# Four 32-partition DMAs in place of one broadcast load, and four in place of one store, in a decoder layer's delta-rule stage

## The chip, the cores and the metric

One core of a Trainium2 chip. The metric is the device time of one execution in microseconds (us), lower is better. The program is one decoder layer for a prompt of 4096 tokens and eight decode tokens. The engines are PE (matrix multiply), DVE (vector), ACT (scalar), POOL, and SP, which here does nothing but issue DMAs. Sixteen DMA engines carry them.

## The reference, cut to what matters

The part that the change touches is the chunked gated delta rule of the prompt. For each chunk and head a unit lower triangular system is solved:

```python
lower = eye + beta[..., :, None] * jnp.einsum('nbhtd,nbhid->nbhti', k, k) * dec_strict
rhs = jnp.concatenate([(beta * jnp.exp(G))[..., None] * k, beta[..., None] * v], -1)
sol = lax.linalg.triangular_solve(lower, rhs, left_side=True, lower=True, unit_diagonal=True)
...
def step(s, xs):
    w_c, ut_c, aqk_c, qd_c, kd_c, gl_c = xs
    u = ut_c - jnp.einsum('bhcd,bhde->bhce', w_c, s)
    o = jnp.einsum('bhcd,bhde->bhce', qd_c, s) + jnp.einsum('bhti,bhie->bhte', aqk_c, u)
    s = gl_c[..., None, None] * s + jnp.einsum('bhcd,bhce->bhde', kd_c, u)
    return s, o
```

Around it stand a projection of the input, a short convolution, sliding-window attention, an output projection and a layer norm.

## The kernel before

The prompt is cut into 16 blocks of 256 tokens. A first phase runs over the blocks (loop variable `s`) and does the projections of q, k and v of the delta heads (PE tile `pj`, w in `w1`), the convolution (DVE, L315, into `kqv` and `vv`), the decay factors (`g`, `dec`), the triangular inverses and the recurrent state `S`. A second phase does attention, gates, output projection and layer norm; it has no instruction of the lines that the change touches.

In the first phase a block has two chunks of 128 tokens and four heads, so eight triangular matrices of 128 x 128. `front` writes them, with sign and decay, into the tile `U` (L379). Their inverses are made in two steps. `lanes` inverts the 32 diagonal sub-blocks of 32 x 32 (four in each matrix) by substitution on DVE, and `gdn_inv` puts the full inverses together from them with matrices on PE (tiles `pgi`, `V`, `XE`, `XZ`). `gdn_c` then updates `S`, through `r` (L491), `ut` (L503) and `S` (L508).

`lanes` works as follows. Four DMAs (L411) store the diagonal sub-blocks to a DRAM buffer `D1` of 32 rows (one for a sub-block, called a lane) and 4 KB. One DMA (L413) reads it back into the tile `LU` of 128 partitions. It reads the 32 rows four times: partitions 0 to 31 hold copy 0 of the 32 lanes, 32 to 63 copy 1, and so on. Each copy solves for a quarter of the 32 columns. `LV` starts as the matching columns of the identity (L415), and 31 steps of a multiply (L420, into `lt`) and an add (L422, into `LV`) do the substitution. One DMA (L424) stores `LV` to the DRAM buffer `D2`, and four DMAs (L429) load its parts as diagonal sub-blocks into `VTd`, from which L432 (ACT) and L433 (DVE) make the halves `vt16` for `gdn_inv`. In the trace `D1` and `D2` both read as `D`. All DMAs of this phase are issued by SP, in one order.

The text is written block after block, but the order of the instructions on each engine is set at build time by a scheduler, which mixes the substitution of one block with the projections of the next, the state update of the block before, and side work (weights for the second phase: `stg`, `wt`, `stt`, and the decode tokens: `stg`, `dkq`, `dt`). An engine runs its own list in that order, so an instruction that waits holds up what stands behind it. Each DMA signals on one of eight semaphores, which are used in turn.

Of the kernel before, what the change touches and what calls it, by code (L numbers as in the profile page):

```python
# [33 lines left out]
def body(ctx, tc, I, O, seq):  # L34
# [3 lines left out]
    pe, act, dve, pool, sp = nc.tensor, nc.scalar, nc.vector, nc.gpsimd, nc.sync  # L38
# [72 lines left out]
    with ExitStack() as p1:  # L111
# [148 lines left out]
        def front(s, hT, ahead):  # L260
# [109 lines left out]
            for c in range(2):  # L370
                cs = slice(c * 128, (c + 1) * 128)
                for hp in range(2):
# [8 lines left out]
                    m = 4 * c + 2 * hp  # L381
                    dve.tensor_mul(Aqk[:, m:m + 2, :], pa[:, :, 0, :], decs[c][:, 2 * hp:2 * hp + 2, :])
            vt, vt16 = lanes(s, U)
            act.activation(U16[:, 0], U, AF.Copy)
            dve.tensor_sub(U16[:, 1], U, U16[:, 0])
# [19 lines left out]
        def lanes(s, U):  # L405

            d1, d2 = D1[s % 2], D2[s % 2]
            d1v = d1.rearrange("(m b) (i t) -> b i m t", b=4, t=32)
            for b in range(4):
                bs = slice(32 * b, 32 * b + 32)  # L410
                sp.dma_start(d1v[b], U[bs, :, bs])  # L411
            LU = w1p.tile([128, 32, 32], F32, name="LU", bufs=1)
            sp.dma_start(LU.rearrange("p a b -> p (a b)"), d1[None].to_broadcast([4, 32, 1024]))  # L413
            LV = w1p.tile([128, 8, 32], F32, name="LV", bufs=1)
            dve.tensor_copy(LV.rearrange("p a b -> p (a b)"), lv0)  # L415
            lt = w1p.tile([128, 8, 32], F32, name="lt", bufs=1)
            for j in range(31, 0, -1):
                j0 = j // 4
                n = 8 - j0
                dve.tensor_mul(lt[:, j0:, 0:j], LV[:, j0:, j:j + 1].to_broadcast([128, n, j]),  # L420
                               LU[:, None, 0:j, j].to_broadcast([128, n, j]))
                dve.tensor_add(LV[:, j0:, 0:j], LV[:, j0:, 0:j], lt[:, j0:, 0:j])  # L422
            d2w = d2.rearrange("l (j c i) -> c l j i", c=4, i=32)
            sp.dma_start(d2w, LV)  # L424
            d2r = d2.rearrange("(m b) (q i) -> b q m i", b=4, i=32)
            vt = VTd
            for b in range(4):
                bs = slice(32 * b, 32 * b + 32)
                sp.dma_start(vt[bs, :, bs], d2r[b])  # L429
            vt16 = w1p.tile([128, 2, 8, 2, 32], F16, name="vt16")  # L430
            ve = vt.rearrange("p m (a b) -> p m a b", b=64)[:, :, :, 0:32]
            act.activation(vt16[:, 0], ve, AF.Copy)  # L432
            dve.tensor_sub(vt16[:, 1], ve, vt16[:, 0])  # L433
            return vt, vt16
# [1020 lines left out]
```

## Time and profile before

| | us |
|---|---|
| median of three runs | 2308.78 (2307.01 to 2318.52) |
| the profiled execution | 2309.84 |
| its span, first to last instruction | 2308.1 |
| PE busy, whole span | 2119.3 |
| DVE busy, whole span | 1834.1 |
| ACT busy, whole span | 1266.6 |
| first phase, steady part | 90 to 1170 of the span |

The profile names each group of instructions as tile written, arrow, tiles read. Idle time of an engine stands in brackets before the instruction that ended it, with the one that released it. A DMA's time in the chain of waits runs from the start of its issue to its landing (of several, from the last one's). The DMA share is the mean busy share of the 16 DMA engines, so 0.25 is four of them.

### The profile page before, as it was taken

Reading aid. Unit: us, or ns where it says so; the run is one execution under the profiler, and the core shown is the slowest. Engines: PE = TensorE matmul, PEld = TensorE weight load, DVE = VectorE, ACT = ScalarE, POOL = GpSimd, SP = SyncE. Lnnn points to the kernel's source line nnn. Section 1 sums busy time; section 2 is a strip of 40 time slices with the busy share of each in tenths; the row PEclk is TensorE's granted clock in tenths of the full one; section 3 lists DMA queues with packets and bytes.
Section 4 is the critical chain, followed back from the end, with each engine's and each line's share of the span. In section 5 each row is a group of like instructions: output and inputs, shape, how many; then the busy total and the mean of one; then the engine's idle time right before and its main releaser. Section 6 shows DMA issues by size and latency. Waiting matters only on the chain.

```text
span 2308.1 us, 48753 instructions
## 1 busy us (share of the span) xinstructions
PE 2119.3 (92%) x18287; PEld 1516.0 (66%) x18287; DVE 1834.1 (79%) x5546; ACT 1266.6 (55%) x3601; POOL 162.0 (7%) x284
## 2 busy tenths in 40 slices
PE   6988798898989898899899999999999999999997
PEld 4867677787877787787576777777545454444443
DVE  7778677888888788888767977777687788898877
ACT  6755656666666576666455666666632333434332
POOL 1111110111111011110000000000000000000000
PEclk9999999999999999999899999999999999999999
DMA  8332322323333123222334311111342343333322
GB/s 321 117 114 67 88 88 72 101 89 94 124 101 98 60 76 99 77 67 79 97 102 165 113 59 63 58 59 39 125 169 74 115 141 105 115 106 111 108 91 74
DMA packets 139757, 232.18 MB, mean 101 GB/s; under 512 B 60933, under 2 KB 73529, under 8 KB 133353
## 3 DMA queue, kind: packets, MB, share of 16 engines
q1 hardware_dynamic: 138224, 228.52, 29.5%
q8 instruction: 144, 2.36, 0.4%
q14 instruction: 93, 0.75, 0.1%
q10 hardware_dynamic: 1296, 0.55, 0.1%
HBM read 154.07 MB, written 76.09 MB: 100 GB/s over the span
## 4 chain that ended last, share of the span: by engine, by line
PE 42%; DVE 17%; DMA 7%; ACT 6%; issue 2%; SPq 1%; POOL 0%; POOLq 0%; ACTq 0%; DVEq 0%
PE pp L1040 21%; PE pj L41 9%; DMA LU<-D 3%; PE pgi L41 3%; DVE kqv L315 2%; ACT Sm L870 2%; PE po L41 2%; DVE lt L420 2%; PE tr L887 2%; DVE LV L422 1%; PE tr L41 1%; PE pS L41 1%; DMA D<-LV 1%; DVE bst L1075 1%; PE pga L41 1%
## 5 line engine op out<-in xcount | busy, mean ns | idle before, releaser
L41 PE MATMUL pj<-hT,w 128*128 128x256 f16 x4608 | 578.8, 276 | 3.4 <-ACT hT L255 2.6
L41 PEld LDWEIGHTS <-w 128*128 128x128 f16 x4800 | 452.8, 99 | 62.2 <-issue 6.8
L1040 PEld LDWEIGHTS <-S 128*128 128x128 f16 x1536 | 150.4, 99 | 170.7 <-issue 3.6
L41 PEld LDWEIGHTS <-hT 128*128 128x128 f16 x2048 | 159.8, 98 | 69.3 <-issue 2.0
L41 PE MATMUL pj<-wq,hT 128*128 128x512 f16 x768 | 191.8, 379 | 0.0
L315 DVE SCALAR_TENSOR_TENSOR kqv<-u,cols,kqv 128x256 f32<-128x256 f32 x384 | 181.4, 478 | 2.7 <-ACT kqv L313 2.1
L1040 PE MATMUL pp<-wz,S 128*128 128x512 f16 x768 | 181.1, 382 | 0.0
L870 ACT ACTIVATE Sm<-Sm,nm 128x256 f32<-128x256 f32 (+1 forms) x256 | 125.5, 492 | 92.4 <-DVE nm L867 92.3
L1040 PE MATMUL pp<-wo,S 128*128 128x512 f16 x768 | 171.3, 379 | 0.7 <-DVE zs L1216 0.6
L420 DVE TENSOR_TENSOR lt<-LV,LU 128x60 f32<-128x60 f32 (+24 forms) x496 | 119.4, 241 | 54.9 <-DMA LU<-D 48.8
L1040 PE MATMUL pp<-wz,hT 128*128 128x512 f16 x576 | 133.0, 382 | 1.2 <-ACT zs L1127 1.2
L863 DVE CUSTOM_DVE_ANT_0 Sm<-pS,swam 128x256 f32<-128x256 f32 (+1 forms) x256 | 96.4, 415 | 35.5 <-PE tr L887 32.0
L1040 PE MATMUL pp<-wo,A 128*128 128x512 f16 x540 | 122.1, 379 | 0.0
L41 PE MATMUL pj<-wkv,hT 128*128 128x256 f16 x768 | 107.7, 275 | 0.4 <-ACT v L814 0.4
L1040 PEld LDWEIGHTS <-hT 128*128 128x128 f16 x612 | 60.1, 99 | 72.7 <-issue 4.4
L422 DVE TENSOR_TENSOR LV<-LV,lt 128x60 f32<-128x60 f32 (+24 forms) x496 | 102.6, 207 | 6.2
L41 PE MATMUL pga<-kqv 128*128 128x256 f32 x256 | 75.3, 409 | 25.7 <-DVE kqv L322 25.7
L1079 POOL TENSOR_TENSOR rs<-rs,cf 128x1 f32<-128x1 f32 (+1 forms) x33 | 22.8, 692 | 1077.1 <-DVE rs L1078 1077.1
L1040 PEld LDWEIGHTS <-A 128*128 128x128 f16 x540 | 52.9, 99 | 62.0
L1021 ACT ACTIVATE S<-zt 128x512 f16<-128x512 f32 x64 | 40.2, 630 | 85.3 <-DVE zt L1027 81.1
L1134 ACT ACTIVATE zs<-zs 128x512 f32<-128x512 f32 x48 | 30.2, 629 | 100.5 <-DVE zs L1133 100.5
L315 DVE SCALAR_TENSOR_TENSOR vv<-u,cols,vv 128x256 f32<-128x256 f32 x192 | 82.6, 479 | 1.7 <-ACT vv L313 0.9
(378 smaller groups left out, 4607.0 us busy)
## 6 DMA issues: line engine op xcount, KB each, us to landing
hT<-hD SPq DMA_DIRECT2D x32, 1024.0 KB
x<-in_xT_dram SPq DMA_DIRECT2D x32, 512.0 KB
hD<-hT SPq DMA_DIRECT2D x16, 1024.0 KB
x<-in_x_prompt_dram SPq DMA_DIRECT2D x60, 256.0 KB
out_y_prompt_dram<-x SPq DMA_DIRECT2D x60, 256.0 KB
stg<-in_ws_dram SPq DMA_DIRECT2D x16, 512.0 KB
LU<-D SPq DMA_DIRECT2D x16, 512.0 KB
wS<-wt SPq DMA_DIRECT2D x16, 512.0 KB
```

The lines of the kernel that those rows point to most:

```text
L41: pe.matmul(out, l, r, start=st, stop=sp_)
L315: dve.scalar_tensor_tensor(d, u[:, b2, j:j + 256], cwj(j, blk), d, op0=ALU.mult, op1=ALU.add)
L420: dve.tensor_mul(lt[:, j0:, 0:j], LV[:, j0:, j:j + 1].to_broadcast([128, n, j]), LU[:, None, 0:j, j].to_broadcast([128, n, j]))
L422: dve.tensor_add(LV[:, j0:, 0:j], LV[:, j0:, 0:j], lt[:, j0:, 0:j])
L863: dve.tensor_tensor_reduce(Sm[:, h, k0:256], pS[:, h2, k0:256], swam[:, k0:256], 0.125, -1e30, op0=ALU.add, op1=ALU.max, accum_out=mx[:, h ...
L870: act.activation(Sm[:, h, k0:256], Sm[:, h, k0:256], AF.Exp, bias=nm[:, h:h + 1], accum_out=sm_[:, h:h + 1])
L887: pe.transpose(pt[:, h2, kb, :], Sm[:, h + h2, kb * 128:(kb + 1) * 128], ident)
L1021: act.activation(q[:, 0], src, AF.Copy)
L1040: pe.matmul(dst.rearrange("p (u c) -> p u c", c=128), A[:, hi, k, :], W[:, k // 2::2, q, wi, k % 2, :], start=new and n == 0, stop=n == 11 ...
L1075: dve.bn_stats(st[0:n, q, :], r[q][0:n])
L1079: pool.tensor_tensor(rs[0:n, 1:2], rs[0:n, 0:1], half_neg[0:n, 0:1], op=ALU.pow)
L1134: act.activation(zs, zs, AF.Silu, scale=IWS)
```

## The change

The load of `LU` and the store of `LV` each become a loop over the four copies, which issues a DMA for 32 partitions. The bytes and their places stay as they were.

```diff
             LU = w1p.tile([128, 32, 32], F32, name="LU", bufs=1)
-            sp.dma_start(LU.rearrange("p a b -> p (a b)"), d1[None].to_broadcast([4, 32, 1024]))
+            for c in range(4):
+                sp.dma_start(LU[32 * c:32 * c + 32].rearrange("p a b -> p (a b)"), d1)
...
             d2w = d2.rearrange("l (j c i) -> c l j i", c=4, i=32)
-            sp.dma_start(d2w, LV)
+            for c in range(4):
+                sp.dma_start(d2w[c], LV[32 * c:32 * c + 32])
```

Lines behind L413 move down by one, those behind L424 by two. The count of compute instructions stays; SP issues 96 DMAs more (three for the load and three for the store in each of 16 blocks). The scheduler's order changes on all engines in the first phase. In the steady part of the second it stays.

On SP, in block 11 (the one whose load stands at 858.49 us in the trace), this is the list from the store of block 10 to the load of block 11, before (`D_0_88` is `D2` of an even block, `D_1_87` is `D1` of an odd one):

```order
L424 DMA D_0_88<-LV 4x256x32
L429 DMA VTd<-D_0_88 32x8x32 x4
L411 DMA D_1_87<-U 32x8x32 x4
L413 DMA LU<-D_1_87 128x1x1024
L136 DMA x<-in_xT_dram 128x1024
```

and after:

```order
L426 DMA D_0_88<-LV 256x1x32 x4
L431 DMA VTd<-D_0_88 32x8x32 x4
L411 DMA D_1_87<-U 32x8x32 x4
L414 DMA LU<-D_1_87 32x1024 x4
L683 DMA out_delta_s_dram<-stg 128x4x128
```

The neighbours stay; one load and one store have become four each.

On DVE, the end of the list between block 11's last instruction on `U` (L379, followed by L382) and the first step of its substitution, before:

```order
L322 SCALAR_TENSOR_TENSOR vv<-th,vv 128x1024
L451 TENSOR_TENSOR VR<-V,VR 64x256
L451 TENSOR_TENSOR V_319<-pgi,V_319 64x256
L668 TENSOR_TENSOR ddl<-ddl,dbe 128x4
L669 TENSOR_TENSOR dt_12648<-xt,deg 128x4
L670 TENSOR_TENSOR doT<-ddl,dqk 128x4
L256 TENSOR_TENSOR hT<-x,hT 128x512
L671 TENSOR_TENSOR doT<-doT,dt_12648 128x4
L256 TENSOR_TENSOR hT<-x,hT 128x512
L451 TENSOR_TENSOR XZ<-pgi,XZ 64x4x64
L420 TENSOR_TENSOR lt<-LV,LU 128x31
L256 TENSOR_TENSOR hT<-x,hT 128x512
```

and after:

```order
L552 SCALAR_TENSOR_TENSOR stg<-stg,xt 128x512
L562 TENSOR_TENSOR stt<-stg 128x256
L453 TENSOR_TENSOR VR<-V,VR 64x256
L453 TENSOR_TENSOR V_319<-pgi,V_319 64x256
L562 TENSOR_TENSOR stt<-stg,stt 128x256
L562 TENSOR_TENSOR stg<-stg 128x256
L562 TENSOR_TENSOR stt<-stg,stt 128x256
L256 TENSOR_TENSOR hT<-x,hT 128x512
L453 TENSOR_TENSOR XZ<-pgi,XZ 64x4x64
L256 TENSOR_TENSOR hT<-x,hT 128x512
L493 SCALAR_TENSOR_TENSOR r<-pgi,G,Vn 128x128 x4
L421 TENSOR_TENSOR lt<-LV,LU 128x31
```

Side work (`stg`, `stt`) and the four instructions on `r`, which stood behind the first step, now stand ahead of it.

On DVE, from the last step of that substitution to the copy that starts the next `LV`, before:

```order
L422 TENSOR_TENSOR LV<-LV,lt 128x8
L315 SCALAR_TENSOR_TENSOR kqv<-u,cols,kqv 128x256 x3
L360 TENSOR_SCALAR sse<-sse 128x8
L361 TENSOR_SCALAR sc<-sse 128x8
L363 RECIPROCAL sc<-sse 128x8
L364 TENSOR_TENSOR sc<-be,sc 128x8
L365 TENSOR_SCALAR sc<-sc 128x8
L315 SCALAR_TENSOR_TENSOR kqv<-u,cols,kqv 128x256
L415 COPY LV<-cf 128x256
```

and after:

```order
L423 TENSOR_TENSOR LV<-LV,lt 128x8
L322 SCALAR_TENSOR_TENSOR kqv<-th,kqv 128x1024
L315 SCALAR_TENSOR_TENSOR vv<-u,cols,vv 128x256 x6
L379 SCALAR_TENSOR_TENSOR U<-pga,sc,dec 128x128 x2
L382 TENSOR_TENSOR Aqk<-pga,dec 128x256
L416 COPY LV<-cf 128x256
```

The convolution steps on `kqv` have moved in between the substitution's steps, and the copy has moved behind the first instructions on the next block's `U`.

## Rows read from the trace of the kernel before

**Rows 1.** Windows: length, then busy us of each engine, PE clock, DMA share, GB/s.

```profile
90.00:1170.00 1080.00, 953.73 (x9351) 820.55 (x9349) 885.43 (x3090) 668.64 (x2147) 125.11 (x224) 0.95 0.29 90
```

**Rows 2.** The chain that ended last, from 90 to 1170 us, shares by line.

```profile
by line: DMA LU<-D 6.9%; DVE kqv L315 5.3%; PE pgi L41 5.1%; DVE lt L420 3.6%; PE pj L41 3.5%; DVE LV L422 3.1%; DMA D<-LV 2.2%; issue 2.1%; PE pga L41 1.9%; DMA D<-U 1.4%; DVE wt L557 1.3%; DVE kqv L322 1.0%; SPq L411 0.7%; DVE S L508 0.7%
```

**Rows 3.** DVE's waits, 90 to 1170 us: total us, times, longest.

```profile
DVE lt L420 <- DMA LU<-D: 48.8, 14, 7.3
...
DVE LV L415 <- DMA D<-LV: 11.4, 5, 3.2
```

**Rows 4.** PE's waits, 90 to 1170 us.

```profile
PE pga L41 <- DVE kqv L322: 24.8, 15, 3.6
PE tr L41 <- DVE g L283: 19.0, 12, 2.0
PE pgi L41 <- DVE r L491: 15.2, 4, 8.6
```

**Rows 5.** SP's timeline: start us, us, issue.

```profile
586.07 0.53 SPq L413 DMA_DIRECT2D LU<-D  x1
...
650.65 0.55 SPq L413 DMA_DIRECT2D LU<-D  x1
...
855.35 1.78 SPq L411 DMA_DIRECT2D D<-U  x4
858.49 0.54 SPq L413 DMA_DIRECT2D LU<-D  x1
864.24 0.35 SPq L136 DMA_DIRECT2D x<-in_xT_dram  x1
...
993.52 0.54 SPq L413 DMA_DIRECT2D LU<-D  x1
...
1059.30 0.54 SPq L413 DMA_DIRECT2D LU<-D  x1
```

**Rows 6.** The chain that ended last, blocks 11 and 14: start us, us, piece.

```profile
856.68 1.67 DMA D<-U
...
858.49 9.41 DMA LU<-D
...
906.67 4.74 DMA D<-LV
...
1059.30 8.42 DMA LU<-D
```

**Rows 7.** Windows as in rows 1: block 14's load of LU.

```profile
1059.30:1060.80 1.50, 1.47 (x14) 1.25 (x14) 1.44 (x3) 0.73 (x2) 0.00 (x0) 1.00 0.06 14
1060.80:1062.30 1.50, 1.42 (x20) 0.91 (x18) 1.47 (x4) 1.20 (x4) 0.00 (x0) 1.00 0.24 71
...
1066.80:1068.30 1.50, 0.80 (x13) 0.51 (x11) 0.56 (x3) 0.40 (x2) 0.00 (x0) 1.00 0.02 8
```

**Rows 8.** Windows as in rows 1: block 11's four stores of U on the way.

```profile
856.60:857.10 0.50, 0.50 (x14) 0.49 (x13) 0.50 (x2) 0.50 (x3) 0.00 (x0) 1.00 0.40 66
```

**Rows 9.** DVE's timeline: first steps of four blocks' substitution, and the copy of LV.

```profile
247.00 0.21 DVE L420 TENSOR_TENSOR lt<-LV,LU 128x31 f32<-128x31 f32 x1 [7.26 <-DMA LU<-D]
391.88 0.21 DVE L420 TENSOR_TENSOR lt<-LV,LU 128x31 f32<-128x31 f32 x1 [4.88 <-DMA LU<-D]
596.20 0.21 DVE L420 TENSOR_TENSOR lt<-LV,LU 128x31 f32<-128x31 f32 x1 [4.08 <-DMA LU<-D]
867.92 0.21 DVE L420 TENSOR_TENSOR lt<-LV,LU 128x31 f32<-128x31 f32 x1 [2.63 <-DMA LU<-D]
911.43 0.29 DVE L415 COPY LV<-cf 128x256 f32<-128x256 f32 x1 [1.23 <-DMA D<-LV]
1002.42 0.21 DVE L420 TENSOR_TENSOR lt<-LV,LU 128x31 f32<-128x31 f32 x1 [1.25 <-DMA LU<-D]
```

**Rows 10.** PE's timeline behind block 11's two stalls.

```profile
869.27 1.93 PE L41 MATMUL pgi<-r,V 128*128 128x128 f32 x8 [2.02 <-DVE r L491]
915.32 1.13 PE L41 MATMUL pga<-kqv 128*128 128x256 f32 x4 [1.65 <-DVE kqv L322]
```

## The prediction

> **What bounds the kernel now.** First the place. The changed lines run only in the first phase, so I read the views from 90 to 1170 us alone. There PE is busy 953.7 of 1080 us and DVE 885.4 [rows 1]: neither is full. PE's 126 idle us (1080 - 953.7) are all that the end can gain while the amount of work and the clock stay.
>
> Second, who is late. The chain that ended last gives 6.9% of this stretch, 75 us, to the load of LU, and 2.2%, 24 us, to the store of LV [rows 2]. At the durations of one, told below, that is about eight of the sixteen loads and five of the stores: in the others something else was later. DVE's largest wait is for the load of LU, 48.8 us in 14 stalls, longest 7.3; it waits 11.4 us in five stalls for the store [rows 3]. PE's largest waits are for DVE: 24.8 us for kqv, 19.0 for g, 15.2 for r, 59.0 together [rows 4].
>
> Third, one block. In block 11 the four stores of U are issued from 855.35 on, LU's load from 858.49 to 859.03, and it lands 9.41 us after its issue began [rows 5, 6]. DVE has other work until 2.63 us before the landing, then stands; PE stands 2.02 us for r, which is behind that first step in DVE's list [rows 9, 10]. At the substitution's end the store takes 4.74 us from issue to landing [rows 6]; DVE waits 1.23 us of it at the copy into LV, and PE a little later 1.65 us for kqv, which is behind that copy [rows 9, 10].
>
> **The change part by part.**
>
> *The load.* Now it costs 9.41 us from the start of its issue to its landing in block 11, 8.42 in block 14 [rows 6]. Block 14's has little beside it: the DMA share is 0.24 from 1060.8 on and the load is over soon after 1066.8 [rows 7]. So four of sixteen engines carry it, for about 6.0 us of data; the other 2.4 are issue, start and completion. The access has four copies outermost, one for each of these engines.
>
> After, four pieces have 32 partitions outermost. The nearest rows are the four stores of U, also 32 partitions each: the last is issued 856.68 - 855.35 = 1.33 us after the first and lands 1.67 us after that [rows 5, 6], with a share of 0.40 on the way, so more than four engines [rows 8]. Low end: all engines carry the data, 6.0/4 = 1.5 us, a quarter of it behind the last issue: 1.33 + 1.67 + 0.4 = 3.4 us. Middle: only 0.40 of the engines, 6.0 x 0.25/0.40 = 3.8 us of data, with the 2.4 of before 6.2 us. High end: no engine is gained, 9.4 + 1.3 = 10.7 us. I take 4 to 4.5, near the low end, because a piece of LU has 32 runs of 4 KB, where the stores of U have short ones: a saving of 5 (at 6.2 us still 3.2).
>
> The Trainium skill, page "DMA: Bandwidth & Descriptors", section "Why a DMA increments its semaphore by 16 and not by 1", says that a DMA runs on the largest number of engines up to 16 that divides the outermost sizes of both sides. That gives four for the old load, as the share of 0.25 shows, and sixteen for each piece; no run here has yet shown the sixteen. By it alone the load would cost the low end's 3.4 us.
>
> What the saving is worth on DVE: a stall can give back no more than itself. The longest, 7.26 us, keeps 2.3; the next, 4.88, and the other twelve go [rows 9]. That is 48.8 - 2.3 = 46.5 us; with a saving of 3.2 it would be about 39. The new order puts side work and the four r instructions ahead of the first step, which covers even the slow price; I add nothing for it, since the load is in time without it.
>
> *The store.* Now 4.74 us. After, four issues and a landing like the stores of U: 1.33 + 1.67 to 2, so 3.2 us, 1.5 saved. The new order also puts kqv, six convolution steps and the next U between the last step and the copy into LV. I count 8 of the 11.4 us of rows 3; the bounds are none and all.
>
> *SP.* 96 more issues at 0.45 are 43 us of SP's time. They cost nothing here: after block 11's load SP issues nothing until 864.24 [rows 5], and the store, like the loads of VTd behind it, waits for the substitution and not for SP. If that cover were gone, the three further issues of the load would hold the DMA behind them back by 1.35 us.
>
> *The order.* The substitution's first steps stand later on DVE, its last step stands closer to the next block's U, and the half vt16 (L435) has moved behind more of the U instructions. Count and kind of compute instructions stay, so this has no price of its own; it can only make waits (rival below).
>
> *The sum.* DVE is freed of 46.5 + 8 = 54.5 us. PE's recoverable time is the 59.0 us for which it names a late DVE. The end gains only where the one falls into the other. In block 11 it does: stalls of 2.63 + 1.23 on DVE, and right behind them 2.02 + 1.23 (of the 1.65) on PE, 84%. But PE's wait for r comes in four blocks of sixteen only [rows 4], and the periods speak for less: the block with a stall of 4.08 takes 650.65 - 586.07 = 64.6 us, one with a stall of 1.25 takes 1059.30 - 993.52 = 65.8 [rows 5, 9]. So between none and 54.5 I take 0.6, 33 us. Profiled execution: its own time of 2309.8 - 33 = 2276.8; the median of three runs stands 1.1 below that execution, so 2276 is predicted. Clock changes are left out: it was 0.95 in this stretch, and I have no row that ties it to these stalls.
>
> **The rivals.**
>
> *Hidden.* The freed DVE time is given back as waits for PE, which is busy 88% of the stretch as it is [rows 1]. For it: the two periods above. Against it: PE's largest waits all name DVE. Gain 10 us or less, about 2302.
>
> *No more engines.* The pieces run as slowly as the one load did, or the four readers of one 4 KB row wait for each other at the source. Then the load is at 10.7 us, 1.3 later, and the new order's cover takes that up: 2305 to 2312. Against it: the 0.40 in rows 8.
>
> *One after the other.* A piece begins only when the one ahead is done. With 2.4 us of issue, start and completion and 0.4 of data each, the load is 4 x 2.8 = 11.2 us, and the store 4 x 1.7 = 6.8, 2 more than now. The load's 1.8 more lie under the new cover; the store's 2 on every block, behind which copy, VTd and inverse wait, give 16 x 2 x 0.6 = 19 at the most, so about 2320. It decides from the point where the pieces land more than some 2 us apart. Against it: the stores of U land 1.67 us after the last issue, so their starts and completions overlap. The same page of the Trainium skill, section "Rules for kernel authors", says not to split a transfer by partitions, because the parts serialize on the same engines, and to use one 128-partition transfer. The trace shows no such thing for the four stores of U.
>
> *A late inverse.* This is slower than before. The substitution now ends closer to the next U, and behind it come store, load of VTd, vt16 and the matrices of the inverse, on which r and S of the block wait. From the substitution's last step to VTd's landing I count 3.2 for the store and as much as the stores of U, 3.0, for the four loads: 6.2 us. If DVE and PE reach vt16 and the inverse before that, a new stall stands where LU's was. At 5 us for each block (more than the 3.5 mean of LU's stalls), and the same weight: 0.6 x (80 - 54.5) = +15, about 2324. It decides from 3.5 us for each block on. Against it: the copy into LV is covered now, and DVE has two or three more groups on U to do before vt16.
>
> **How the numbers follow.** Half a percent, 11.5 us, is about what a measurement of this kernel tells from no change. Chances: my forecast 0.70 (2245 to 2297), hidden 0.16, no more engines 0.04, one after the other 0.04, a late inverse 0.06. The lower end of the range, 2240, is all of the 54.5 us and some more of the chain's 99; the upper, 2307, leaves out the two slower cases and a part of the hidden one's scatter. Faster is 0.70 and a little of the hidden case, 0.71; slower is 0.10 with the last two, less what of them stays within the bound, 0.09; same is the rest, 0.20.
>
> **What would show each step.** Right: LU<-D in the chain at 1.7 to 3 us for its last piece instead of 9.4, a DMA share far over 0.25 while it lands, DVE's wait for LU under 5 us in total, D<-LV at about 2 us, PE's waits for g, kqv and r clearly below 59. Wrong: a DVE wait for LU of the old size (engines), or no such wait with PE's waits unchanged in sum (hidden), or a new row at vt16, XE or V in DVE's waits of over 50 us (late inverse). If the first phase gets shorter by much more than 54.5 us, the clock or the order did it, and my sum has missed its cause.

## The result and the profile after

| | us | |
|---|---|---|
| before, median of 4 runs | 2309.13 | 2307.01 to 2318.52 |
| after, median of 4 runs | 2236.32 | 2233.91 to 2240.11 |
| ratio, 95% interval | 0.968 | 0.965 to 0.971 |
| after, profiled execution | 2235.32 | span 2233.5 |

The kernel became faster by 73 us, more than twice the 33 us of the forecast and 3.7 us below the lower end of its range. Where did it come from? I cut the span where SP issues its first `wz<-wS`, a load of the second phase's weights that all kernels here have. It stands at 1204.94 us before and at 1134.84 us after. Two stretches up to it, and the one behind it up to the first issue of `wo<-wS`, follow as windows with the columns of rows 1 (length; busy us of PE, of PE's weight loads, of DVE, ACT and POOL, each with its count of instructions; PE clock, DMA share, GB/s). First the kernel after:

```profile
90.00:1100.00 1010.00, 933.60 (x9316) 801.26 (x9314) 878.93 (x3082) 668.63 (x2149) 126.68 (x224) 0.98 0.30 96
...
90.00:1134.84 1044.84, 967.54 (x9660) 827.38 (x9658) 903.77 (x3159) 686.28 (x2212) 129.70 (x227) 0.98 0.30 95
...
1134.84:1582.95 448.11, 436.02 (x4852) 312.63 (x4851) 339.49 (x1271) 281.32 (x843) 0.00 (x0) 0.99 0.21 79
```

The kernel before, for the last two:

```profile
90.00:1204.94 1114.94, 987.86 (x9692) 845.72 (x9690) 908.31 (x3163) 685.55 (x2211) 128.24 (x227) 0.96 0.29 89
...
1204.94:1658.57 453.63, 437.73 (x4835) 314.09 (x4833) 338.94 (x1269) 280.54 (x844) 0.00 (x0) 0.98 0.22 78
```

The first stretch of rows 1 (up to 1170, now up to 1100) does nearly the same work: 9351 PE instructions before [rows 1], 9316 now. Up to `wz<-wS` the phase is shorter by 1114.94 - 1044.84 = 70.1 us. PE's idle time there fell from 127.1 (1114.94 - 987.86) to 77.3 us (1044.84 - 967.54), which is 49.8 us. The other 20.3 us are PE's *busy* time, 987.86 against 967.54 at a granted clock that went from 0.96 to 0.98. The instructions recorded, 9692 and 9660, differ by 0.3%, which is some 3 us of it at the most. Behind the cut 5.5 us more are gained (453.63 - 448.11), 3.8 of them less idle PE. Together that is 75.6 us; the spans differ by 2308.1 - 2233.5 = 74.6, so in what lies outside both stretches 1.0 us is lost.

The chain that ended last, from 90 to 1100 us, beside rows 2 (the view cuts the line off):

```profile
by line: PE pgi L41 12.2%; DVE kqv L315 11.4%; PE pj L41 11.0%; DVE lt L421 6.7%; PE pga L41 6.0%; DVE LV L423 5.6%; issue 4.2%; DVE kqv L322 2.9%; PE xt L41 2.8%; DVE vv L315 2.1%; DMA x<-in_xT_dram 2.1%; ACT junk L392 1.8%; PE tr L389 1.6
```

No load of LU and no store of LV is left in it, behind the cut-off either. DVE's largest waits of the same stretch (total, times, longest) say it too:

```profile
DVE U L379 <- PE pga L41: 30.4, 30, 2.7
DVE kqv L322 <- ACT th L321: 8.6, 9, 1.2
...
DVE vt L435 <- ACT vt L434: 3.4, 4, 2.0
```

The two rows of rows 3, 48.8 and 11.4 us, are gone to the last. What grew is DVE's wait for PE at `U`, from 14.0 us to 30.4: a part of the freed time was given back there. The rows of before for `U` and for the half of the inverse `vt`, from 90 to 1170 us:

```profile
DVE U L379 <- PE pga L41: 14.0, 11, 2.6
...
DVE vt L433 <- ACT vt L432: 6.6, 8, 1.3
```

PE's waits of after answer to rows 4:

```profile
PE pga L41 <- DVE kqv L322: 23.2, 15, 2.3
PE tr L41 <- DVE g L283: 10.1, 8, 2.8
...
PE pgi L41 <- ACT V L452: 4.9, 10, 1.8
```

PE's wait for `r`, 15.2 us before, is no longer among the largest, and the one for `g` is halved. Rows 4 show the three largest only: all rows of that view in which PE waits for DVE sum to 96.4 us before and to 48.9 us now, and that fall of 47.5 is nearly all of the 49.8 us of idle time. Now block 11 closely, the one of rows 5 and 6. SP's timeline:

```profile
795.75 1.78 SPq L411 DMA_DIRECT2D D<-U  x4
798.87 1.71 SPq L414 DMA_DIRECT2D LU<-D  x4
801.80 0.40 SPq L683 DMA_DIRECT2D out_delta_s_dram<-stg  x1
...
846.27 2.52 SPq L426 DMA_DIRECT2D D<-LV  x4
850.19 1.82 SPq L431 DMA_DIRECT2D VTd<-D  x4
```

And windows over the load, beside rows 7:

```profile
798.80:799.80 1.00, 0.99 (x18) 0.77 (x16) 0.97 (x4) 0.23 (x1) 0.00 (x0) 1.00 0.00 0
799.80:800.80 1.00, 0.97 (x13) 0.67 (x10) 0.97 (x3) 0.73 (x2) 0.19 (x1) 1.00 0.84 266
800.80:801.80 1.00, 1.00 (x26) 0.76 (x24) 0.97 (x5) 0.97 (x2) 0.00 (x0) 1.00 0.93 250
801.80:802.80 1.00, 1.00 (x6) 0.78 (x6) 1.00 (x1) 1.00 (x4) 0.00 (x0) 1.00 0.13 26
```

The data run for 2 us at a share of 0.84 to 0.93, where the one load of before ran for 6 us at 0.24 [rows 7]; about 3 us behind the first issue (798.87 to some 801.8) they are over. DVE comes to the first step only 9 us later:

```profile
809.84 1.13 DVE L493 SCALAR_TENSOR_TENSOR r<-pgi,G,Vn 128x128 f32<-128x128 f32 x4
810.88 0.20 DVE L421 TENSOR_TENSOR lt<-LV,LU 128x31 f32<-128x31 f32 x1
```

There is no bracket of idle time at the step (beside rows 9), and PE's matrices on `r` start at 810.77 without one (beside rows 10). With 12.0 us from first issue to the step, even the 9.41 us of before would have been in time in this block; whether the order or the load took the stalls away has to be tried.

### The profile page after: what moved, and what is told of

The parts are those of the page before. It is cut to its first block, busy times and chain, and to the rows that moved or that the text cites. A ratio compares the mean times of both kernels' runs of the same rounds, so it can differ in the third digit from the quotient of the medians.

```text
span 2233.5 us, 48900 instructions
## 1 busy us (share of the span) xinstructions
PE 2098.6 (94%) x18287; PEld 1497.6 (67%) x18287; DVE 1831.9 (82%) x5546; ACT 1269.1 (57%) x3601; POOL 163.4 (7%) x284
## 4 chain that ended last, share of the span: by engine, by line
PE 53%; DVE 28%; ACT 11%; DMA 4%; issue 3%; POOL 0%; POOLq 0%; SPq 0%; ACTq 0%; DVEq 0%
PE pp L1042 21%; PE pj L41 11%; PE pgi L41 6%; DVE kqv L315 5%; DVE lt L421 3%; PE pga L41 3%; ACT Sm L872 3%; DVE LV L423 3%; PE po L41 2%; PE tr L41 2%; PE tr L889 2%; DMA x<-in_xT_dram 1%; DVE kqv L322 1%; PE xt L41 1%; PE pS L41 1%
## 5 line engine op out<-in xcount | busy, mean ns | idle before, releaser
L41 PEld LDWEIGHTS <-w 128*128 128x128 f16 x4800 | 450.0, 99 | 65.1 <-issue 11.4
```

Source lines behind the costliest of these rows:

```text
L41: pe.matmul(out, l, r, start=st, stop=sp_)
```

## The experiments

My theory at that point: the load was slow because its outermost size of 4 gave it four engines, DVE's stalls on it and on the store stopped PE, and the clock fell behind these stops. The rivals: the new order of the instructions did it; the store did it; the number of DMAs did it, not the engines. All six kernels, called e1 to e6 here, compute the whole reference. The first four ran beside a before of 2309.81 us (13 runs), the last two beside one of 2308.87 us (7 runs).

**One half of the change each.** First (e1) only the load is split.

```diff
+            for c in range(4):
+                sp.dma_start(LU[32 * c:32 * c + 32].rearrange("p a b -> p (a b)"), d1)
...
             sp.dma_start(d2w, LV)
```

> Only the load of LU is split into four DMAs of 32 partitions; the store of LV stays one DMA. Theory 'engines' (each piece runs on all DMA engines, so the load is short and DVE's stall for it goes): DVE's wait for LU under 5 us in sum, the load's last piece 1.7 to 3 us in the chain, time 2245 to 2265 us, most of the 73 us. Theory 'order' (the build-time order that four issues bring puts more work ahead of the first substitution step, whatever the load's speed): a time in the same region, so this run tells the two apart only together with the third. Theory 'store' (the store's part is worth as much as the load's): 2270 to 2285.

Measured: 2240.19 us, 0.968 of before (0.966 to 0.971). Windows and DVE's waits of this kernel:

```profile
90.00:1138.43 1048.43, 966.96 (x9686) 825.70 (x9685) 905.82 (x3164) 688.52 (x2212) 125.75 (x227) 0.99 0.30 94
```

```profile
DVE LV L416 <- DMA D<-LV: 4.2, 4, 1.8
```

By its ratio this is the gain of after (0.968 and 0.968); the 4 us between the two medians are not clear of the noise. The store, left as it was, costs DVE 4.2 us of waits and not 11.4. Then (e2) only the store is split.

```diff
             sp.dma_start(LU.rearrange("p a b -> p (a b)"), d1[None].to_broadcast([4, 32, 1024]))
...
+            for c in range(4):
+                sp.dma_start(d2w[c], LV[32 * c:32 * c + 32])
```

> Only the store of LV is split; the load of LU stays one DMA with four copies outermost. 'Engines': DVE's wait for LU stays near 49 us in sum, its wait for the store goes, time 2290 to 2304 us. 'Order': the order of the first phase is another one here too, so the time may come out anywhere from 2240 to 2310 with the load as slow as before. 'Store': 2270 to 2285.

Measured: 2293.65 us, 0.9923 (0.9902 to 0.9945).

```profile
90.00:1191.53 1101.53, 984.48 (x9646) 844.95 (x9644) 905.11 (x3151) 686.14 (x2207) 124.06 (x227) 0.95 0.28 89
```

```profile
DVE lt L420 <- DMA LU<-D: 47.8, 14, 5.8
```

The store's wait is gone and LU's is what it was, 47.8 against 48.8 us. So the store's split, with the order that comes with it, is worth 16 us alone, and 4 us or less behind the load's split: the two share their gain. This kernel's instruction order is another one than those of before and after, and it did not take LU's stalls away here.

**Four DMAs without more engines (e3).** The load is cut into four by columns, so that each piece still has the four copies outermost; the store is one DMA.

```diff
+            for c in range(4):
+                sp.dma_start(LU[:, 8 * c:8 * c + 8].rearrange("p a b -> p (a b)"),
+                             d1[None, :, 256 * c:256 * c + 256].to_broadcast([4, 32, 256]))
```

> The load of LU is split into four DMAs, but by columns: each still has four copies outermost, 128 partitions and 1 KB runs. The store stays one DMA. 'Engines': a DMA share of 0.25 while it lands, the load at 9 to 12 us from the first issue, DVE's wait for LU 15 to 60 us in sum, time 2285 to 2320 us. 'Order': with four issues as in the run with the load alone, the time is that run's, within 10 us.

Measured: 2300.76 us, 0.9961 (0.9945 to 0.9977). Windows of the phase and of block 11's load, and DVE's waits:

```profile
90.00:1193.10 1103.10, 983.16 (x9691) 840.99 (x9690) 907.48 (x3163) 685.87 (x2211) 132.22 (x227) 0.96 0.28 90
...
855.00:857.00 2.00, 1.98 (x26) 1.54 (x24) 1.94 (x7) 1.82 (x6) 0.00 (x0) 1.00 0.24 48
```

```profile
DVE lt L422 <- DMA LU<-D: 34.7, 14, 6.0
DVE LV L417 <- DMA D<-LV: 12.8, 6, 3.2
```

The share stays at 0.24, and the load lands 9.1 us behind its first issue (851.53 to 860.64). Four DMAs in flight together, each with four copies outermost, use no more engines than one, and DVE stalls 14 times as before. The wait is 14 us shorter than before, and the time 9 us; that its order covers a little more is likely, and was not tried. So it is not the count of the DMAs.

**One DMA with more engines (e4).** The opposite: one load of 128 partitions, but with the 32 lanes outermost and the copies inside. Partition 4l + c then holds copy c of lane l, so the host's table of the identity's columns and the store's source follow; the store stays split.

```diff
+            sp.dma_start(LU.rearrange("p a b -> p (a b)"), d1[:, None, :].to_broadcast([32, 4, 1024]))
...
+                sp.dma_start(d2w[c], LV[c::4])
...
+            lane[p, jj, 4 * jj + p % 4] = 1.0
```

> The load of LU is one DMA again, but with 32 lanes outermost and the four copies inside (partition 4*lane + copy; the identity's table and the store's four DMAs, of every fourth partition, follow). 'Engines': one issue, all engines, the load at 2.5 to 4 us from issue to landing, DVE's wait for LU under 5 us, time 2225 to 2250 us. 'Order': with one issue the order is nearer to the old one, and the time is nearer to that of the run with the store alone, 2280 us or more.

Measured: 2242.36 us, 0.970 (0.968 to 0.972).

```profile
90.00:1133.84 1043.84, 967.29 (x9653) 829.66 (x9651) 905.42 (x3153) 684.42 (x2208) 127.97 (x227) 0.97 0.29 94
...
804.00:805.00 1.00, 0.95 (x10) 0.73 (x9) 0.98 (x1) 0.44 (x3) 0.00 (x0) 1.00 0.60 152
805.00:806.00 1.00, 1.00 (x23) 0.87 (x22) 0.96 (x4) 0.87 (x2) 0.00 (x0) 1.00 0.93 356
806.00:807.00 1.00, 0.99 (x19) 0.66 (x16) 1.00 (x5) 0.98 (x4) 0.00 (x0) 1.00 0.08 33
```

One DMA, issued at 803.05, reaches 0.93 too, and the first phase is as short as that of after, 1043.84 against 1044.84 us. DVE waits for LU once, 2.2 us, in a block whose load is issued right behind a load of `x` (868.18 and 868.71) and lands 7.1 us later. The kernel's median is 6 us behind that of after, with intervals of the ratio that overlap; in the profiled executions the difference lies behind the cut, 1133.84 to 1591.90 being 458.06 us where after takes 448.11. The code there is the same, and I did not follow it further.

This run says more together with e2. Both have one DMA for the load and four for the store, and the traces of the two list the same instructions in the same order on every engine: 18287 on PE, 5546 on DVE, 3601 on ACT, 284 on POOL, 749 DMAs on SP. What differs is the load's access, which 32 partitions each of the store's DMAs reads, and the values in the host's table. So here the order is held fixed, and with it the load alone is worth 2293.65 - 2242.36 = 51.3 us. The theory 'Order' expected 2280 us or more.

**Half of the engines (e5).** The prediction's disputed number is what a stall is worth at the end. So the load is made worse: two DMAs with two copies outermost each; the store is one DMA. From the first four kernels I had 0.85 us of PE idle for each us of DVE's DMA waits.

```diff
+            for c in range(2):
+                sp.dma_start(LU[64 * c:64 * c + 64].rearrange("p a b -> p (a b)"),
+                             d1[None].to_broadcast([2, 32, 1024]))
```

> The cost under suspicion doubled: the load of LU is two DMAs of 64 partitions, each with two copies outermost, so two engines should carry all of it; the store stays one DMA. 'Engines': a DMA share of 0.12 while it lands, the load at 13 to 16 us from the first issue, DVE's wait for LU 85 to 130 us in sum. PE's idle time to the issue of wz has so far followed DVE's two DMA waits at 0.85 us for one (77 us with none, 127 us with 60): then 160 to 200 us here, a clock of 0.95 or less, and a time of 2345 to 2400 us. If the time of the changed kernel came from the order of the instructions and not from the load, this run lies within 15 us of 2310.

Measured: 2371.12 us, 1.027 (1.024 to 1.031). Windows of the phase, of block 11's load and of what is behind it; then DVE's waits:

```profile
90.00:1264.36 1174.36, 1000.34 (x9680) 857.43 (x9679) 907.24 (x3162) 685.29 (x2211) 135.74 (x227) 0.93 0.26 84
...
829.00:831.00 2.00, 0.00 (x0) 0.00 (x0) 0.00 (x0) 0.00 (x0) 0.00 (x0) 1.00 0.13 53
831.00:833.00 2.00, 0.00 (x0) 0.00 (x0) 0.09 (x1) 0.00 (x0) 0.00 (x0) 1.00 0.14 50
833.00:834.00 1.00, 0.00 (x0) 0.00 (x0) 1.00 (x3) 0.25 (x1) 0.00 (x0) 0.60 0.12 51
834.00:835.00 1.00, 0.62 (x3) 0.63 (x4) 1.00 (x4) 1.00 (x3) 0.00 (x0) 0.50 0.37 127
...
838.00:840.00 2.00, 2.00 (x11) 2.00 (x11) 1.81 (x7) 1.35 (x7) 0.00 (x0) 0.50 0.11 42
```

```profile
DVE lt L422 <- DMA LU<-D: 90.6, 14, 9.0
DVE LV L417 <- DMA D<-LV: 15.2, 8, 2.6
```

A share of 0.13 is two of sixteen engines; the load lands 14.7 us behind its first issue (818.13 to 832.81). From 829 to nearly 833 us no engine computes at all; PE stands 5.5 us, to 834.4, and when it begins again its granted clock is 0.50, the lower level of 1.2 GHz, and still is at 840. PE's idle time in the phase is 174.0 us (1174.36 - 1000.34). PE's busy time rose to 1000.3, at a clock of 0.93.

**An order in favour of the substitution (e6).** With the load fast, the scheduler is told to put the 31 steps first wherever they are ready.

```diff
+            with tc.high_priority():
+                for j in range(31, 0, -1):
```

> The changed kernel with its 31 substitution steps given priority in the build-time order: the same DMAs and the same instructions in another order, the steps denser and earlier. If the order by itself carries little, as the runs so far suggest, 2225 to 2250 us with PE idle at 70 to 85 us to the issue of wz. If the new order was what made the gain, the time may leave that region by more than 20 us. A gain of over 10 us would be a better version.

Measured: 2229.05 us, 0.966 of before (0.963 to 0.969). Its median is the lowest here, 7 us below that of after; each has a before of its own, 2308.87 and 2309.13, and the intervals of the two ratios overlap.

```profile
90.00:1124.67 1034.67, 965.29 (x9703) 829.15 (x9701) 898.95 (x3168) 684.46 (x2212) 125.75 (x227) 0.98 0.30 96
```

PE idles 69.4 us, 8 less than after, with busy time and clock practically the same. The phase is 10.2 us shorter than that of after. So this order in favour of the substitution is worth some 10 us of the phase, and by its time it is not clear of the noise; the load at a fixed order is worth 51.

**All kernels side by side**, the phase from 90 us to `wz<-wS`, idle being length less busy, from the windows and waits above:

| kernel | load's engines | DVE waits, LU + store | PE idle | PE busy | clock |
|---|---|---|---|---|---|
| e5 | 2 | 90.6 + 15.2 | 174.0 | 1000.3 | 0.93 |
| before | 4 | 48.8 + 11.4 | 127.1 | 987.9 | 0.96 |
| e2 | 4 | 47.8 + 0 | 117.1 | 984.5 | 0.95 |
| e3 | 4 | 34.7 + 12.8 | 119.9 | 983.2 | 0.96 |
| e1 | all | 0 + 4.2 | 81.5 | 967.0 | 0.99 |
| after | all | 0 + 0 | 77.3 | 967.5 | 0.98 |
| e4 | all | 2.2 + 0 | 76.6 | 967.3 | 0.97 |
| e6 | all | 0 + 0 | 69.4 | 965.3 | 0.98 |

The four kernels with a slow load stand apart from the four with a fast one in LU's waits, PE idle, PE busy and clock, whatever their order. The pair e2 and e4, with the same order, shows that the load alone does it: phase 57.7 us shorter, PE idle 40.5 less, PE busy 17.2 less, for 45.6 us less of DVE's waits. What of the 73 us is the store's and what the order's is not separated.

## Why the prediction was right and wrong

**The mechanism: right.** Four copies outermost hold the load to four engines; 32 outermost let it use nearly all. The share went from 0.24 to 0.84 and more, the load's data from about 6.0 us to 2, over about 3 us behind the first issue, and e3 and e4 show that it is the outermost size and not the count of DMAs; e2 and e4, with the same order, show that it makes the time. The rule of the Trainium skill, page "DMA: Bandwidth & Descriptors", section "Why a DMA increments its semaphore by 16 and not by 1", agrees: two engines in e5 (0.13), four in e3 (0.24), up to sixteen in after (0.93).

**DVE's stalls: 46.5 and 8 us were counted, 48.8 and 11.4 went.** In block 11 the data are over some 2.9 us behind the first issue; before, in block 14, the landing came at 1067.7, less than 1 us behind the data [rows 6, 7], so the 4 to 4.5 us that I took for the load fits. The longest stall, 7.26 us [rows 9], did not keep its 2.3; the work that the new order puts ahead of the first step is a likely reason, which I did not try. The store went to 850.19 - 846.27 = 3.9 us up to the issue that waits for it, not 3.2: its four issues take 2.52 us, where those of the stores of U take 1.78 [rows 5]; I had counted the 1.33 up to the start of their last. Its wait on DVE went all the same.

**The step that failed: in "The sum", "So between none and 54.5 I take 0.6, 33 us", and with it "a stall can give back no more than itself".** Three things were wrong with it: the weight, the time that PE could win back, and the clock.

First the weight. PE's idle time fell by 49.8 us for 60.2 us of DVE waits, 0.83. e2 gives (117.1 - 77.3)/47.8 = 0.83, e3 0.90 and e5 (174.0 - 77.3)/105.8 = 0.91; e2 against e4, at the same order, gives 40.5/45.6 = 0.89. I had 0.84 in hand from block 11's own stalls (that one block comes so close to the mean of all is in part luck) and threw it away for two block periods. That comparison was worth nothing. SP's timeline of after, the loads of LU of three successive blocks:

```profile
478.44 1.71 SPq L414 DMA_DIRECT2D LU<-D  x4
...
541.31 1.72 SPq L414 DMA_DIRECT2D LU<-D  x4
...
611.38 1.71 SPq L414 DMA_DIRECT2D LU<-D  x4
```

The periods here are 62.9 and 70.1 us and no block has a stall on LU: what else the scheduler puts into a block moves its period by 7.2 us, as much as the longest stall.

Second the time that PE could win back. In the prediction's "PE's recoverable time is the 59.0 us for which it names a late DVE" the 59.0 are the three rows shown; all of PE's waits for DVE were 96.4 us, so there was more to win back than the sum said.

Third the clock, which the prediction left out by name. Behind block 11's stall in the kernel before, as windows:

```profile
867.00:868.00 1.00, 0.24 (x3) 0.05 (x1) 0.08 (x1) 0.72 (x3) 0.00 (x0) 1.00 0.45 139
868.00:869.00 1.00, 0.00 (x0) 0.00 (x0) 0.97 (x3) 0.42 (x2) 0.00 (x0) 1.00 0.03 12
869.00:870.00 1.00, 0.73 (x4) 0.76 (x5) 1.00 (x6) 0.60 (x1) 0.00 (x0) 0.70 0.37 156
870.00:871.00 1.00, 1.00 (x7) 1.00 (x7) 1.00 (x1) 0.00 (x0) 0.00 (x0) 0.50 1.10 434
871.00:872.00 1.00, 1.00 (x6) 1.00 (x6) 0.90 (x3) 0.00 (x0) 0.00 (x0) 0.50 1.06 344
872.00:873.00 1.00, 1.00 (x8) 0.78 (x7) 0.53 (x4) 0.91 (x4) 0.00 (x0) 0.59 0.80 164
873.00:874.00 1.00, 1.00 (x12) 0.98 (x10) 0.60 (x3) 1.00 (x3) 0.00 (x0) 1.00 0.93 328
```

PE stands 2 us, and then works for some 3 us at or near half of its clock. I had looked at this very stall [rows 10] without reading the clock column behind it. Over the phase the fall in busy time of 20.3 us fits this. By the trace's record of the granted clock, it stands at 0.50 for 99.0 us of the phase before, in which PE is busy 81.8, and for 44.4 us after, in which PE is busy 38.6. Eight matrices `pgi<-ut,Kd` take 2.08 us at 0.50 (e5, at 834.38) and 1.06 at 1.00 (before, at 873.31). So about half of these busy times is what the clock costs by this estimate, 40.9 and 19.3 us, and the difference is 21.6. The 20.3 us are a third of DVE's waits (20.3/60.2 = 0.34; in e5 (1000.3 - 967.5)/105.8 = 0.31; e2 against e4 17.2/45.6 = 0.38). So a microsecond of DVE's waits cost the phase 70.1/60.2 = 1.16 us, in e5 (1174.36 - 1044.84)/105.8 = 1.22, e2 against e4 57.7/45.6 = 1.27: a stall gave back more than itself. With 0.83 + 0.34 in place of 0.6, the 54.5 us of the prediction would have been 64.

The clock does not fall behind every stall. In the 5 us behind the 14 stalls on LU the clock is below 1.00 in eight cases and 1.00 in six, two of them being

```profile
247.00:252.00 5.00, 1.24 (x6) 1.12 (x7) 3.25 (x16) 4.01 (x18) 1.01 (x1) 0.50 0.17 66
...
660.90:665.90 5.00, 2.96 (x57) 2.80 (x58) 4.89 (x13) 2.85 (x9) 0.00 (x0) 1.00 0.21 67
```

and in one of the eight it had fallen before the stall. So the price of the clock holds for the sum of many stalls and not for each. That it falls for the stalls rests on its place behind them, on its going with the waits in eight kernels, and on e2 and e4, where the order is the same and only the load is slower; I did not hold the clock still to try it apart.

**The rivals.** *Hidden* holds in part: DVE waits 16 us more for `pga` than before, but PE's idle time fell. *No more engines* falls by the share; e3 is the kernel that does what this rival said, at 2300.76 us. *One after the other* falls: the data of four pieces run for 2 us in one piece of time. The highest time that its sum allows would have been 2309 + 19 = 2328 us, where the prediction says 2320. The rule of the Trainium skill, page "DMA: Bandwidth & Descriptors", section "Rules for kernel authors", that two transfers to disjoint halves of the partitions are not worth it, has as its reason that both use all 16 engines; the one load here used four (0.24), so the split paid. In e4, where one DMA reaches 0.93, it makes the phase as short as four. *A late inverse* falls: DVE's wait at `vt` went from 6.6 to 3.4 us.

**My own sentence on a gain far above 54.5 us**, that the clock or the order did it, proved half right: the clock did a good quarter of the 70.1 us (20.3), the stalls most of the rest; e6's new order at a fast load moved the phase by 10 us. What is left open is the 5.5 us behind the cut. The kernels scatter there between 448 us (after) and 458 us (e4), so it is not the load alone.

## What to carry to other kernels

Read the DMA share while a slow transfer is alone on the way: 0.25 says four engines of sixteen, and the outermost size of the access, above all a broadcast of few copies put outermost, is the place to look; putting the long dimension outermost does as well as splitting. When you price a stall on an engine that feeds PE, take the weight from PE's idle time right behind such stalls, and from all of PE's waits that name that engine, and not from periods of whole blocks, and read the granted clock in the microseconds after it, since PE may come back at half speed and the stall then costs more than its length. Expect two such waits on one path to share their gain: the store's split was worth 16 us alone and 4 us or less behind the load's. Where every edit reshuffles the instructions, compare the lists of the kernels that you have: two that agree in every list but differ in the transfer, as e2 and e4, tell the transfer from the order.

## What the runs showed of the hardware that was not expected

Several DMAs issued one behind the other with few copies outermost do not spread over different engines: four with four copies each stay at a share of 0.24 (e3), two with two copies each at 0.13 (e5), as one would. Four issues do not cost SP the same everywhere: 2.52 us for the stores of LV, 1.78 for those of U, 1.71 for the loads of LU; what makes the difference was not tried. And the granted clock fell to 0.50 behind a stop of PE of only 2.0 us (before, at 869.27), and was back at 1.00 less than 4 us after PE had begun again, while a stop of 2.9 us that ended at 662.94 left it at 1.00; behind e5's stop of 5.5 us it was still at 0.50 after 5.6 us of work.
